# Gate and up projection of a decoder layer: column groups two at a time, with seven block products in place of eight in some units

## Chip, core and metric

One core of one Trainium2 chip runs the whole layer. The metric is the device time of one execution in microseconds (us), the median of several runs.

## What is computed

One decoder layer for 256 tokens with a model width of 2048, all in float32: a convolution branch and an attention branch, their joint output projection, and a gated feed-forward part.

```python
mix = concat([rmsnorm(u, conv_out_norm), rmsnorm(attn, attn_out_norm)]) @ w_out
x = x + rmsnorm(mix, post_mix_norm)
hf = rmsnorm(x, pre_ffn_norm)
ff = (silu(hf @ w_gate) * (hf @ w_up)) @ w_down      # 2048 -> 5632 -> 2048
x = x + rmsnorm(ff, post_ffn_norm)
```

## The kernel before

The 256 tokens are two token blocks (tb) of 128. Every float32 operand of a product is held as two float16 parts, hi and lo, and a product of one 128-row tile with 512 columns is three matmuls: hi times hi, hi times lo, lo times hi. A weight tile of 128x2048 float32 (1 MB) is loaded by SyncE's queue (SP) into one of 4 buffers `st`; `split` (L98 to L100) lets ScalarE write the hi part `whi` (L99) and then VectorE the lo part `wlo` (L100). The parts have 8 buffers each in the pool `wsp`. The tile framework fixes in advance the order in which each engine's instructions stand; an engine takes them in that order, so an instruction that waits holds up all behind it.

The output projection of the convolution half (L588 to L595) ends with x for the next part. For each tb, L601 adds the residual, L602 squares it for the norm, L604 forms x times the gain, L606 splits that, and L607 transposes the parts by DMA into `hf`. The norm's factor `r_f` (L610 to L612) is not in `hf`: it is applied to the product, as a scale in `swiglu` (L640, L645).

The gate and up projection (L661 to L677) has 22 column groups j of 512 columns (256 of gate, 256 of up) and 16 row tiles. A group's weights are 4 loads, its products 96 matmuls into two accumulators of the pool `acc` (4 PSUM banks). The first two groups do tb 0 before tb 1. `swiglu` computes silu(gate) times up, and splits and transposes it into `aT`. For the groups in `FAST` (0, 2, ..., 18) it also forms three differences of blocks, `sT`, for the down projection.

The down projection (L737 to L802) has 22 pairs of row tiles and two halves of 1024 columns. A pair is one load of four blocks, and a plain pair has eight block products (2 tb x 2 column groups x 2 row tiles, 24 matmuls). Ten pairs take seven (21 matmuls), the Strassen-Winograd form: the weights' four sums are formed in place on VectorE (L730 to L732) and split again, so VectorE has for such a pair a split of 128x1536, three additions and a split of 128x2048. Four products go into the pool `tmp` (the other 4 banks) and are added at the end of a half (L778 to L786). Fast and plain pairs alternate.

```python
nc.vector.tensor_tensor(st[:, 0:4:3, :], st[:, 0:2, :], st[:, 3:4, :].to_broadcast([P, 2, 512]), op=ALU.add)
nc.vector.tensor_tensor(st[:, 1, :], st[:, 0, :], st[:, 1, :], op=ALU.add)
nc.vector.tensor_tensor(st[:, 2, :], st[:, 1, :], st[:, 2, :], op=ALU.add)
return parts + parts_of(st, 2048)
```

Of the kernel before, what the change touches and what calls it, by code (L numbers as in the profile page):

```python
# [17 lines left out]
P = 128  # L18
# [33 lines left out]
def hymba_layer(ctx: ExitStack, tc: tile.TileContext, x, xT, pos, inv_freq, g_pre, w_in, w_lat,  # L52
# [15 lines left out]
    arena = const.tile([P, 70 * KB], F32, name="arena")  # L68
# [511 lines left out]

    mxc_of = flat(mx_h[:, :CB], mx_l[:, :CB])
    x_off = dram.tile([P, NTB, D], F32, name="x_off")
    r_f = const.tile([P, NTB], F32, name="r_f")
    for tb in range(NTB):
# [13 lines left out]
        for j in range(4):  # L598
# [25 lines left out]
    hw3 = region(50, (2, 3, P), F16)  # L624

# [3 lines left out]
    def fast_of(j):  # L629
# [5 lines left out]
    def swiglu(j, ps):  # L635
        fast = j in FAST
        for tb in range(NTB):
            r = r_f[:, tb : tb + 1]
            sg = work.tile([P, 256], F32, tag="A", name=nm("sg"), bufs=3)
            nc.scalar.activation(sg, ps[tb][:, 0:256], AF.Silu, scale=r)  # L640
# [4 lines left out]
            nc.vector.scalar_tensor_tensor(a, ps[tb][:, 256:512], r, sg, op0=ALU.mult, op1=ALU.mult)  # L645
# [15 lines left out]
    LEAD = 2  # L661
    lead = []
    for j in range(NG):
        wgt = Weights(KD, 512).load(w_gu[j], W_S)
        ps = [acc_tile(), acc_tile()]
        if j < LEAD:
            mm3(ps[0:1], hf_of, wgt, (0,))
            lead.append((wgt, ps))
            if j == LEAD - 1:
                for i, (wgt, ps) in enumerate(lead):  # L670
                    mm3(ps[1:2], hf_of, wgt, (1,))
                    swiglu(i, ps)
# [44 lines left out]
    def parts_of(st, n):  # L717
        hi = wsp.tile([P, 2048], F16, tag="whi", name=nm("whi"))
        lo = wsp.tile([P, 2048], F16, tag="wlo", name=nm("wlo"))
        split(hi[:, :n], lo[:, :n], st.rearrange("p b n -> p (b n)")[:, :n], WD_S)  # L720
        return [(hi[:, c : c + 512], lo[:, c : c + 512]) for c in range(0, n, 512)]

    def load_pair(u, i):

        st = stage.tile([P, 2048], F32, tag="stage", name=nm("st")).rearrange("p (b n) -> p b n", b=4)
        nc.sync.dma_start(st, w_dn[u, i])
        if i not in FAST:
            return parts_of(st, 2048)
        parts = parts_of(st, 1536)
        nc.vector.tensor_tensor(st[:, 0:4:3, :], st[:, 0:2, :], st[:, 3:4, :].to_broadcast([P, 2, 512]), op=ALU.add)  # L730
        nc.vector.tensor_tensor(st[:, 1, :], st[:, 0, :], st[:, 1, :], op=ALU.add)
        nc.vector.tensor_tensor(st[:, 2, :], st[:, 1, :], st[:, 2, :], op=ALU.add)  # L732
        return parts + parts_of(st, 2048)

# [150 lines left out]
```

## Time and profile before

| | |
|---|---|
| median of 3 runs | 1015.81 us (1015.81 to 1016.43) |
| profiled execution | 1016.03 us, span 1014.2 us, mean granted TensorE clock 0.991 |
| busy, share of the span | TensorE 96%, VectorE 73%, ScalarE 53% |
| HBM read | 204.25 MB, 206 GB/s over the span |

The span runs from the first to the last instruction; 1.8 us of the time lie around it. Busy shares are means over stages, so the stages have to be read apart: the gate and up projection lies between about 330 and 784 us, the down projection from there to about 1005 us.

### The profile page before, as it was taken

Reading aid. Unit: us, or ns where it says so; the run is one execution under the profiler, and the core shown is the slowest. Engines: PE = TensorE matmul, PEld = TensorE weight load, DVE = VectorE, ACT = ScalarE, POOL = GpSimd, SP = SyncE. Lnnn points to the kernel's source line nnn. Section 1 sums busy time; section 2 is a strip of 40 time slices with the busy share of each in tenths; the row PEclk is TensorE's granted clock in tenths of the full one; section 3 lists DMA queues with packets and bytes.
Section 4 is the critical chain, followed back from the end, with each engine's and each line's share of the span. In section 5 each row is a group of like instructions: output and inputs, shape, how many; then the busy total and the mean of one; then the engine's idle time right before and its main releaser. Section 6 shows DMA issues by size and latency. Waiting matters only on the chain.

```text
span 1014.2 us, 11941 instructions
## 1 busy us (share of the span) xinstructions
PE 975.7 (96%) x4652; PEld 462.3 (46%) x4652; DVE 742.5 (73%) x860; ACT 532.5 (53%) x599; POOL 37.7 (4%) x50
## 2 busy tenths in 40 slices
PE   6999997999999999999999999999999999989996
PEld 2444553774444444444444444444444444434442
DVE  6699999999868886555455555555556788888787
ACT  7796665664746564454444444454443544554551
POOL 0000000034100100000000000000000000000000
PEclk9999998999999999999999999999999999999998
DMA  9874666576546998676766776777755555635453
GB/s 348 330 256 140 223 209 196 166 241 222 201 166 170 321 303 290 218 228 201 240 217 206 222 224 223 226 218 217 234 198 166 176 189 224 235 127 222 166 186 145
DMA packets 77769, 220.37 MB, mean 217 GB/s; under 512 B 49552, under 2 KB 50192, under 8 KB 55184
## 3 DMA queue, kind: packets, MB, share of 16 engines
q1 hardware_dynamic: 76992, 218.68, 64.2%
q10 hardware_dynamic: 720, 0.93, 0.3%
q8 instruction: 36, 0.59, 0.2%
q14 instruction: 21, 0.17, 0.1%
HBM read 204.25 MB, written 4.19 MB: 206 GB/s over the span
## 4 chain that ended last, share of the span: by engine, by line
PE 64%; DVE 18%; issue 5%; ACT 5%; POOL 2%; DMA 1%; DVEq 0%; POOLq 0%; ACTq 0%; SPq 0%
PE acc L146 16%; PE acc L145 16%; PE acc L144 16%; DVE wlo L100 7%; DVE arena L277 3%; PE acc L749 3%; PE acc L750 3%; PE acc L748 3%; ACT whi L99 3%; DVE st L730 1%; PE tmp L749 1%; PE tmp L750 1%; PE tmp L748 1%; POOL sm L198 1%; DVE arena L285 1%
## 5 line engine op out<-in xcount | busy, mean ns | idle before, releaser
L100 DVE SCALAR_TENSOR_TENSOR wlo<-st,whi 128x2048 f16<-128x2048 f32 (+4 forms) x211 | 451.7, 2157 | 203.3 <-ACT whi L99 203.3
L99 ACT ACTIVATE whi<-st 128x2048 f16<-128x2048 f32 (+4 forms) x211 | 376.2, 1800 | 320.7 <-PE acc L146 176.5
L144 PE MATMUL acc<-whi,arena 128*128 128x512 f16 (+1 forms) x1084 | 410.1, 378 | 5.5 <-ACT whi L99 5.5
L145 PE MATMUL acc<-wlo,arena 128*128 128x512 f16 (+1 forms) x1084 | 410.4, 379 | 3.9 <-DVE wlo L100 3.8
L146 PE MATMUL acc<-whi,arena 128*128 128x512 f16 (+1 forms) x1084 | 409.8, 378 | 0.0
L144 PEld LDWEIGHTS <-arena 128*128 128x128 f16 x1084 | 106.7, 98 | 130.2 <-ACT arena L104 4.9
L146 PEld LDWEIGHTS <-arena 128*128 128x128 f16 x1084 | 106.7, 98 | 129.6 <-issue 6.9
L145 PEld LDWEIGHTS <-arena 128*128 128x128 f16 x1084 | 106.5, 98 | 125.2 <-issue 2.5
L748 PE MATMUL acc<-whi,arena 128*128 128x512 f16 x232 | 87.9, 379 | 0.0
L749 PE MATMUL acc<-wlo,arena 128*128 128x512 f16 x232 | 87.9, 379 | 0.0
L750 PE MATMUL acc<-whi,arena 128*128 128x512 f16 x232 | 87.9, 379 | 0.0
L277 DVE SCALAR_TENSOR_TENSOR arena<-arena 128x256 f32<-128x256 f32 x184 | 78.0, 480 | 0.0
L640 ACT ACTIVATE sg<-acc,r_f 128x256 f32<-128x256 f32 x44 | 20.7, 473 | 58.8 <-PE acc L146 58.8
L749 PEld LDWEIGHTS <-arena 128*128 128x128 f16 x272 | 26.6, 98 | 32.3 <-issue 0.3
L748 PEld LDWEIGHTS <-arena 128*128 128x128 f16 x272 | 26.6, 98 | 32.1
L750 PEld LDWEIGHTS <-arena 128*128 128x128 f16 x272 | 26.6, 98 | 32.1
L283 ACT ACTIVATE x_sb<-arena 128x256 f32<-128x256 f32 x56 | 25.2, 506 | 11.7 <-DVE arena L285 11.7
L705 POOL TENSOR_TENSOR sm<-sm,neg_half 128x1 f32<-128x1 f32 x2 | 1.1, 541 | 657.0 <-DVE sm L703 657.0
L730 DVE TENSOR_TENSOR st<-st 128x1024 f32<-128x1024 f32 x20 | 24.5, 1224 | 0.6
L153 PE MATMUL tmp<-arena,whi 128*128 128x256 f16 x80 | 21.8, 273 | 0.0
L154 PE MATMUL tmp<-arena,whi 128*128 128x256 f16 x80 | 21.8, 273 | 0.0
L155 PE MATMUL tmp<-arena,wlo 128*128 128x256 f16 x80 | 21.8, 273 | 0.0
(186 smaller groups left out, 610.1 us busy)
## 6 DMA issues: line engine op xcount, KB each, us to landing
st<-in_w_gu SPq DMA_DIRECT2D x88, 1024.0 KB, 5.0
st<-in_w_dn SPq DMA_DIRECT2D x44, 1024.0 KB, 4.9
st<-in_w_out SPq DMA_DIRECT2D x16, 1024.0 KB, 5.1
st<-in_w_in SPq DMA_DIRECT2D x14, 1024.0 KB, 9.3
st<-in_w_lat SPq DMA_DIRECT2D x12, 896.0 KB, 5.0
x_sb<-in_x SPq DMA_DIRECT2D x4, 1024.0 KB, 8.7
st<-in_w_uqn SPq DMA_DIRECT2D x4, 768.0 KB, 4.9
st<-in_w_uv SPq DMA_DIRECT2D x2, 1024.0 KB, 6.0
```

The lines of the kernel that those rows point to most:

```text
L99: nc.scalar.activation(hi, src, AF.Copy, scale=scale)
L100: nc.vector.scalar_tensor_tensor(lo, src, scale, hi, op0=ALU.mult, op1=ALU.subtract)
L144: nc.tensor.matmul(p_ap, xh, wh, start=(start and k == 0), stop=False)
L145: nc.tensor.matmul(p_ap, xh, wl, start=False, stop=False)
L146: nc.tensor.matmul(p_ap, xl, wh, start=False, stop=(stop and k == wgt.kt - 1))
L153: nc.tensor.matmul(ps, wh[:, c0 : c0 + P], xh, start=(k == 0), stop=False)
L277: nc.vector.scalar_tensor_tensor(cacc[:, cb, :], upad[:, cb, k : k + S], cw[:, cb, k : k + 1], cacc[:, cb, :], op0=ALU.mult, op1=ALU.add)
L283: nc.scalar.activation(t[:, i, :], upad[:, cb, k : k + S], AF.Copy, scale=cw[:, cb, k : k + 1])
L730: nc.vector.tensor_tensor(st[:, 0:4:3, :], st[:, 0:2, :], st[:, 3:4, :].to_broadcast([P, 2, 512]), op=ALU.add)
L748: nc.tensor.matmul(ps, ah, bh, start=key not in begun, stop=False)
L749: nc.tensor.matmul(ps, ah, bl, start=False, stop=False)
L750: nc.tensor.matmul(ps, al, bh, start=False, stop=last)
```

## The change

The gate and up projection takes its 22 column groups in 11 units of two, with weights laid out in blocks as for the down projection. In units 1, 3, 5, 7 and 9, five of the eight pairs of row tiles (0 to 4) take seven block products; pair 5 goes first, then 0 to 4, then 6 and 7. All other units have eight plain pairs. The down projection uses the same class and changes only in that its tail holds two pairs, not three. A unit's four results and, in a fast unit, its four sums fill all eight PSUM banks; units in turn take their results from `acc` and from `tmp`, and their sums from the other pool.

Sums of blocks of the normed input are needed too (`hf_sums`, once, in unit 0), and sums of blocks from two tb have to have the same scale, so the norm's factor now goes into `hf` itself (`normed`): a token block's squares are reduced and raised to the power before the first split.

```diff
+GU_UNITS = (1, 3, 5, 7, 9)
+GU_FAST = 5
...
+    def normed(tb, j):
+        cs = slice(j * 512, (j + 1) * 512)
+        gx = work.tile([P, 512], F32, tag="ss", name=nm("gxf"), bufs=3)
+        nc.vector.scalar_tensor_tensor(gx, x_sb[:, tb, cs], r_f[:, tb : tb + 1], g_pf[:, cs], op0=ALU.mult, op1=ALU.mult)
+        return gx
...
             nc.scalar.activation(junk_tile(512), xs, AF.Square, accum_out=ss4[:, j : j + 1])
-            gx = work.tile([P, 512], F32, tag="ss", name=nm("gxf"), bufs=3)
-            nc.vector.tensor_tensor(gx, xs, g_pf[:, cs], op=ALU.mult)
+        s1 = smalls()
+        nc.vector.tensor_reduce(s1, ss4, axis=AX.X, op=ALU.add)
+        rstd_of(s1, D, out_tile=r_f[:, tb : tb + 1])
+        for j in range(4):
             hl = work.tile([P, 2, 512], F16, tag="hl", name=nm("hl"))
-            split(hl[:, 0, :], hl[:, 1, :], gx, X_S)
+            split(hl[:, 0, :], hl[:, 1, :], normed(tb, j), X_S)
...
+    def hf_sums(c):
+        g0, g1 = [normed(tb, c).rearrange("p (i k t) -> p i k t", i=2, k=2) for tb in range(NTB)]
+        sm = region(44, (4, 2, P))
+        for d, p, m in ((0, g1[:, :, 0], g1[:, :, 1]), (1, g0[:, :, 0], g1[:, :, 0]),
+                        (2, g0[:, :, 0], sm[:, 0]), (3, g0[:, :, 1], sm[:, 2])):
+            nc.vector.tensor_tensor(sm[:, d], p, m, op=ALU.subtract)
+        hl = region(48, (2, 8 * P), F16)
+        split(hl[:, 0, :], hl[:, 1, :], sm.rearrange("p s i t -> p (s i t)"), X_S)
+        nc.sync.dma_start_transpose(hS[:, c], hl.rearrange("p a n -> p (a n)"))
...
+    class Unit:
+        def __init__(self, x_of):
+            mine, other = (acc_tile, tmp_tile) if Unit.count % 2 == 0 else (tmp_tile, acc_tile)
+            Unit.count += 1
+            self.E = [[mine(), mine()], [mine(), mine()]]
...
+        def fast(self, blocks, w, last):
+            if self.sums is None:
+                self.sums = [self.other() for _ in range(4)]
+            X, Y, Z, Q = self.sums
+            A22, A11, A12, S1, S3, S2, S4 = blocks
+            self.mm(self.E[0][0], (0, 0), A12, w[2])
+            self.mm(self.E[0][1], (0, 1), S4, w[1])
+            self.mm(X, "X", A11, w[0], last)
+            self.mm(Y, "Y", S2, w[4], last)
+            self.mm(Z, "Z", S3, w[6], last)
+            self.mm(Q, "Q", S1, w[3], last)
+            self.mm(self.E[1][0], (1, 0), A22, w[5])
+            if last:
+                xs_ = work.tile([P, 512], F32, tag="hl", name=nm("xs"))
+                nc.scalar.copy(xs_, X)
+                m, n_, q2 = [work.tile([P, 512], F32, tag="ss", name=nm(b), bufs=3) for b in ("m", "n", "q2")]
+                nc.vector.tensor_tensor(m, xs_, Y, op=ALU.subtract)
+                nc.vector.tensor_tensor(n_, m, Z, op=ALU.add)
+                nc.vector.tensor_tensor(m, Q, m, op=ALU.subtract)
+                nc.vector.tensor_tensor(q2, Q, n_, op=ALU.subtract)
+                self.fix = [[xs_, m], [n_, q2]]
+        def block(self, tb, c):
+            e = self.E[tb][c]
+            if self.fix is None:
+                return e
+            f = self.fix[tb][c]
+            nc.vector.tensor_tensor(f, e, f, op=ALU.add)
+            return f
...
+    gu_order = [GU_FAST] + list(range(GU_FAST)) + list(range(GU_FAST + 1, KP))
+    for u in range(NU):
+        unit = Unit(hf_of)
+        if u == 0:
+            ws = [load_pair(w_gu[u, i], W_S, False) for i in range(KP)]
+            for tb in range(NTB):
+                for i, w in enumerate(ws):
+                    for c in range(2):
+                        unit.plain(i, w, tb, c, i == KP - 1)
+                if tb == 0:
+                    for c in range((GU_FAST + 1) // 2):
+                        hf_sums(c)
         else:
-            mm3(ps, hf_of, wgt)
-            swiglu(j, ps)
+            order = gu_order if u in GU_UNITS else list(range(KP))
+            for i in order:
+                fast = u in GU_UNITS and i < GU_FAST
+                w = load_pair(w_gu[u, i], W_S, fast)
+                if fast:
+                    unit.fast(hf_fast(i), w, i == GU_FAST - 1)
+                else:
+                    unit.plain_all(i, w, i == order[-1])
+        for c in range(2):
+            swiglu(2 * u + c, unit, c)
...
-    TAIL = 3
+    TAIL = 2
```

`load_pair` and `parts_of` are moved from the down projection unchanged but for the scale; the reduced dynamic DMA scratch makes room for `hS`.

How the order of instructions moves, at three places. First VectorE in the middle of the gate and up projection: before, one column group of 512 (L645 and L655 are in `swiglu`, the rows with arena its splits).

```order
L100 SCALAR_TENSOR_TENSOR wlo_4604<-st_4601,whi_4603 128x2048
L100 SCALAR_TENSOR_TENSOR wlo_4610<-st_4607,whi_4609 128x2048
L100 SCALAR_TENSOR_TENSOR wlo_4616<-st_4613,whi_4615 128x2048
L645 SCALAR_TENSOR_TENSOR arena<-acc_4349,r_f,sg_4447 128x256
L645 SCALAR_TENSOR_TENSOR arena<-acc_4350,r_f,sg_4450 128x256
L655 TENSOR_TENSOR arena<-arena 128x128 x4
L100 SCALAR_TENSOR_TENSOR wlo_4622<-st_4619,whi_4621 128x2048
```

In the change, the end of unit 3's fast pairs (L676 to L678 are the additions that were L730 to L732, L105 the split, L730 and L731 the first steps of adding the four sums):

```order
L105 SCALAR_TENSOR_TENSOR wlo_3982<-st_3979,whi_3981 128x1536
L676 TENSOR_TENSOR st_3979<-st_3979 128x2x512
L677 TENSOR_TENSOR st_3979<-st_3979 128x512
L678 TENSOR_TENSOR st_3979<-st_3979 128x512
L105 SCALAR_TENSOR_TENSOR wlo_3989<-st_3979,whi_3988 128x2048
L105 SCALAR_TENSOR_TENSOR wlo_4016<-st_4013,whi_4015 128x1536
L676 TENSOR_TENSOR st_4013<-st_4013 128x2x512
L677 TENSOR_TENSOR st_4013<-st_4013 128x512
L678 TENSOR_TENSOR st_4013<-st_4013 128x512
L105 SCALAR_TENSOR_TENSOR wlo_4023<-st_4013,whi_4022 128x2048
L105 SCALAR_TENSOR_TENSOR wlo_4059<-st_4056,whi_4058 128x2048
L730 TENSOR_TENSOR m_4049<-xs_4047,acc_3887 128x512
```

Fast pairs stand one behind the other, with nothing between L678 and the split that follows it.

Second, VectorE where the gate and up projection ends and the weights of the down projection are prepared. Before (the accumulators of the last group are acc_5867 and acc_5868):

```order
L100 SCALAR_TENSOR_TENSOR wlo_6092<-st_6089,whi_6091 128x2048
L100 SCALAR_TENSOR_TENSOR wlo_6122<-st_6119,whi_6121 128x1536
L730 TENSOR_TENSOR st_6119<-st_6119 128x2x512
L731 TENSOR_TENSOR st_6119<-st_6119 128x512
L732 TENSOR_TENSOR st_6119<-st_6119 128x512
L645 SCALAR_TENSOR_TENSOR a_5967<-acc_5867,r_f,sg_5965 128x256
L645 SCALAR_TENSOR_TENSOR a_5975<-acc_5868,r_f,sg_5973 128x256
```

In the change (unit 10's results are acc_5919 to acc_5922, L757 is the multiplication of `swiglu`):

```order
L105 SCALAR_TENSOR_TENSOR wlo_6306<-st_6303,whi_6305 128x2048
L105 SCALAR_TENSOR_TENSOR wlo_6336<-st_6333,whi_6335 128x1536
L757 SCALAR_TENSOR_TENSOR a_6165<-acc_5919,sg_6163 128x256
L676 TENSOR_TENSOR st_6333<-st_6333 128x2x512
L105 SCALAR_TENSOR_TENSOR ahl_6167<-a_6165,ahl_6167 128x256
L757 SCALAR_TENSOR_TENSOR a_6173<-acc_5921,sg_6171 128x256
L757 SCALAR_TENSOR_TENSOR a_6181<-acc_5920,sg_6179 128x256
L677 TENSOR_TENSOR st_6333<-st_6333 128x512
L105 SCALAR_TENSOR_TENSOR ahl_6175<-a_6173,ahl_6175 128x256
L757 SCALAR_TENSOR_TENSOR a_6189<-acc_5922,sg_6187 128x256
```

The four reads that free the banks stand behind the split of seven weight tiles of the down projection (wlo_6204 is the first), and its first pair now takes its sums from `acc`, so from these four banks.

Third, VectorE where token block 0 is made ready. Before:

```order
L601 SCALAR_TENSOR_TENSOR x_sb<-arena,sm_2730,x_sb 128x512 x2
L604 TENSOR_TENSOR gxf_2736<-x_sb,arena 128x512
L604 TENSOR_TENSOR gxf_2745<-x_sb,arena 128x512
L601 SCALAR_TENSOR_TENSOR x_sb<-arena,sm_2730,x_sb 128x512 x2
L100 SCALAR_TENSOR_TENSOR hl_2738<-gxf_2736,hl_2738 128x512
```

In the change (L613 is the old L601, L603 the old L591, L616 the reduction of the squares, L590 is in `normed`):

```order
L613 SCALAR_TENSOR_TENSOR x_sb<-arena,sm_2730,x_sb 128x512 x4
L105 SCALAR_TENSOR_TENSOR wlo_2948<-st_2945,whi_2947 128x2048
L603 SCALAR_TENSOR_TENSOR arena<-acc_2776,r_c,arena 128x512
L105 SCALAR_TENSOR_TENSOR wlo_2954<-st_2951,whi_2953 128x2048
L105 SCALAR_TENSOR_TENSOR wlo_2960<-st_2957,whi_2959 128x2048
L616 TENSOR_REDUCE sm_2745<-sm_2732 128x1
L605 TENSOR_TENSOR arena<-arena 128x512
L201 TENSOR_SCALAR sm_2747<-sm_2745 128x1
L603 SCALAR_TENSOR_TENSOR arena<-acc_2805,r_c,arena 128x512
L590 SCALAR_TENSOR_TENSOR gxf_2751<-x_sb,r_f,arena 128x512
```

Three splits of weights and the norm's steps now stand between the finished x and the first normed tile; after this row two more rows of L590 and a fourth split of weights follow before the first `hl`.

## Rows read from the trace of the kernel before

**Rows 1.** The page, busy time of each engine over the span.
```profile
PE 975.7 (96%) x4652; PEld 462.3 (46%) x4652; DVE 742.5 (73%) x860; ACT 532.5 (53%) x599; POOL 37.7 (4%) x50
```

**Rows 2.** Windows: stretch, length, busy us per engine (instructions), PEclk, DMA share, GB/s.
```profile
330.00:351.00 21.00, 19.53 (x92) 8.76 (x91) 18.74 (x25) 10.16 (x18) 3.06 (x2) 1.00 1.02 333
351.00:784.00 433.00, 433.00 (x2008) 196.31 (x2007) 251.28 (x218) 198.39 (x171) 0.00 (x0) 1.00 0.71 227
784.00:892.00 108.00, 108.00 (x502) 48.95 (x501) 89.44 (x68) 52.44 (x35) 0.00 (x0) 1.00 0.53 197
892.00:896.00 4.00, 0.78 (x5) 0.29 (x3) 3.28 (x3) 3.39 (x5) 0.00 (x0) 1.00 0.02 4
896.00:1005.00 109.00, 107.07 (x495) 48.09 (x492) 88.83 (x73) 48.24 (x38) 0.54 (x1) 1.00 0.47 180
400.00:500.00 100.00, 100.00 (x465) 45.36 (x464) 54.58 (x48) 44.78 (x40) 0.00 (x0) 1.00 0.70 219
```

**Rows 3.** Waits, 340 to 735 us: who waited for whom, us, times, longest.
```profile
ACT whi L99 <- PE acc L146: 152.6, 55, 3.5
```

**Rows 4.** TensorE's timeline in the gate and up projection: start, us, what.
```profile
729.76 0.38 PE L144 MATMUL acc<-whi,arena 128*128 128x512 f16 x1
...
772.06 0.38 PE L145 MATMUL acc<-wlo,arena 128*128 128x512 f16 x1
```

**Rows 5.** VectorE's timeline in the down projection, one fast and one plain pair.
```profile
853.38 6.16 DVE L100 SCALAR_TENSOR_TENSOR wlo<-st,whi 128x2048 f16<-128x2048 f32 x3 [2.06 <-ACT whi L99]
859.58 1.23 DVE L730 TENSOR_TENSOR st<-st 128x1024 f32<-128x1024 f32 x1
860.84 0.69 DVE L731 TENSOR_TENSOR st<-st 128x512 f32<-128x512 f32 x1
861.56 0.69 DVE L732 TENSOR_TENSOR st<-st 128x512 f32<-128x512 f32 x1
864.31 10.56 DVE L100 SCALAR_TENSOR_TENSOR wlo<-st,whi 128x2048 f16<-128x2048 f32 x5 [2.06 <-ACT whi L99]
```

**Rows 6.** VectorE's groups by form, 740 to 1000 us: busy us, mean ns.
```profile
L784 DVE TENSOR_TENSOR m<-tmp,m 128x512 f32<-128x512 f32 x2 | 1.4, 686 | 0.1
L686 DVE TENSOR_TENSOR xs<-acc,xs 128x512 f32<-128x512 f32 x2 | 1.4, 688 | 1.0 <-PE acc L750 1.0
```

**Rows 7.** Where the input of the gate projection is made: timelines of VectorE and TensorE.
```profile
309.37 1.42 DVE L601 SCALAR_TENSOR_TENSOR x_sb<-arena,sm,x_sb 128x512 f32<-128x512 f32 x2 [0.66 <-POOL sm L198]
313.23 1.29 DVE L100 SCALAR_TENSOR_TENSOR hl<-gxf,hl 128x512 f16<-128x512 f32 x2
330.15 0.74 DVE L591 SCALAR_TENSOR_TENSOR arena<-acc,r_c,arena 128x512 f32<-128x512 f32 x1
346.65 0.38 PE L145 MATMUL acc<-wlo,arena 128*128 128x512 f16 x1 [1.47 <-DVE wlo L100]
```

**Rows 8.** The tile hl: its transposes by DMA, ns min/median/max on SP, and landing in us.
```profile
L607 SPq DMA_TRANSPOSE arena<-hl x8: 1242/1532/3357, 313.9 to 349.7; - x8
DMA to landing us min/median/max: 3.1/4.1/5.9
```

**Rows 9.** VectorE's timeline where the gate and up projection ends.
```profile
784.46 0.69 DVE L732 TENSOR_TENSOR st<-st 128x512 f32<-128x512 f32 x1
785.07 0.87 DVE L645 SCALAR_TENSOR_TENSOR a<-acc,r_f,sg 128x256 f32<-128x256 f32 x2
```

**Rows 10.** TensorE's timeline after the two longest waits shown.
```profile
163.00 0.47 PE L373 MATMUL tmp<-ident,kp 128*128 128x128 f32 x1 [6.25 <-DVE kp L372]
895.66 0.38 PE L748 MATMUL acc<-whi,x_sb 128*128 128x512 f16 x1 [3.22 <-DVE m L686]
```

**Rows 11.** Windows behind the wait of 6.25 us, columns as in rows 2.
```profile
160.00:165.00 5.00, 2.00 (x6) 0.84 (x7) 3.87 (x18) 4.29 (x10) 1.16 (x2) 0.54 0.42 152
165.00:170.00 5.00, 5.00 (x20) 2.20 (x19) 5.00 (x9) 2.10 (x3) 0.00 (x0) 0.78 0.65 116
```

More of the change, by code (lines that the diff above doesn't have):

```diff
@@ L67, in hymba_layer @@
     KB = 256
-    arena = const.tile([P, 70 * KB], F32, name="arena")
+    arena = const.tile([P, 82 * KB], F32, name="arena")
     def region(kb, shape, dtype=F32):
@@ new lines, in parts_of, with load_pair @@
+    def parts_of(st, n, scale):
+        hi = wsp.tile([P, 2048], F16, tag="whi", name=nm("whi"))
+        lo = wsp.tile([P, 2048], F16, tag="wlo", name=nm("wlo"))
+        split(hi[:, :n], lo[:, :n], st.rearrange("p b n -> p (b n)")[:, :n], scale)
+        return [(hi[:, c : c + 512], lo[:, c : c + 512]) for c in range(0, n, 512)]
+    def load_pair(src, scale, fast):
+        st = stage.tile([P, 2048], F32, tag="stage", name=nm("st")).rearrange("p (b n) -> p b n", b=4)
+        nc.sync.dma_start(st, src)
+        if not fast:
+            return parts_of(st, 2048, scale)
+        parts = parts_of(st, 1536, scale)
+        nc.vector.tensor_tensor(st[:, 0:4:3, :], st[:, 0:2, :], st[:, 3:4, :].to_broadcast([P, 2, 512]), op=ALU.add)
+        nc.vector.tensor_tensor(st[:, 1, :], st[:, 0, :], st[:, 1, :], op=ALU.add)
+        nc.vector.tensor_tensor(st[:, 2, :], st[:, 1, :], st[:, 2, :], op=ALU.add)
+        return parts + parts_of(st, 2048, scale)
@@ new lines, in hymba_layer, with mm, plain, plain_all @@
+    class Unit:
+        count = 0
+        def __init__(self, x_of):
+            mine, other = (acc_tile, tmp_tile) if Unit.count % 2 == 0 else (tmp_tile, acc_tile)
+            Unit.count += 1
+            self.x_of, self.other = x_of, other
+            self.E = [[mine(), mine()], [mine(), mine()]]
+            self.sums = None
+            self.begun = set()
+            self.fix = None
+        def mm(self, ps, key, a, b, last=False):
+            (ah, al), (bh, bl) = a, b
+            nc.tensor.matmul(ps, ah, bh, start=key not in self.begun, stop=False)
+            nc.tensor.matmul(ps, ah, bl, start=False, stop=False)
+            nc.tensor.matmul(ps, al, bh, start=False, stop=last)
+            self.begun.add(key)
+        def plain(self, i, w, tb, c, last=False):
+            self.mm(self.E[tb][c], (tb, c), self.x_of(2 * i, tb), w[0 if c == 0 else 3])
+            self.mm(self.E[tb][c], (tb, c), self.x_of(2 * i + 1, tb), w[2 if c == 0 else 1], last)
+        def plain_all(self, i, w, last=False):
+            for tb in range(NTB):
+                for c in range(2):
+                    self.plain(i, w, tb, c, last)
+        def fast(self, blocks, w, last):
[26 more added lines that the diff above has]
+            return f
@@ L715, in final @@
             (nc.sync if j % 2 == 0 else nc.scalar).dma_start(out[tb * P : (tb + 1) * P, cs], xs)
[L717 to L733, printed above, removed]
@@ L788, in hymba_layer @@
+        unit = Unit(a_of)
+        for i in order[:-TAIL]:
+            w = load_pair(w_dn[u, i], WD_S, i in FAST)
+            if i in FAST:
+                unit.fast(a_fast(i), w, i == FAST[-1])
+            else:
+                unit.plain_all(i, w)
+        tail = [(i, load_pair(w_dn[u, i], WD_S, False)) for i in order[-TAIL:]]
         if u == 1:
```

101 lines of the change are left out of this document (25 added, 76 removed).

## Prediction

> **What bounds the kernel now.** I read the page's busy shares first, then the windows by stage, then who waits for whom in each stage. Over the span TensorE is busy 96% and VectorE 73% [rows 1]; the windows show that this mean hides two kinds of stage [rows 2]. From 351 to 784 us TensorE has no gap, and VectorE is busy 54.58 us of 100: the gate and up projection is paced by TensorE, and ScalarE's hi splits wait for it to give back buffers, 152.6 us in 55 waits [rows 3]. From 784 us on VectorE is busy 89.44 of 108 us. There it also waits 2.06 us in each fast pair for ScalarE: the second hi split can start only when the last addition is done, and nothing else stands between them in VectorE's queue [rows 5]. The cadence of one fast and one plain pair is 864.31 - 853.38 = 10.93 us.
>
> TensorE's price is read from 197 matmuls in a row without a gap, (772.06 - 729.76) / 196 = 0.2158 us each [rows 4]. A plain pair (24) is 5.18 us, a fast pair (21) 4.53, a plain unit of eight 41.4. One fast and one plain pair are 9.71 us, so the down projection's VectorE is already 1.2 us slower per two pairs than its TensorE. It lives on the lead that it brings from the gate and up projection, and one wait for an evacuation shows (3.22 us, [rows 10]). The change carries such pairs to a stage where VectorE had time, and puts five of them in a row. The question is whether there is time enough.
>
> **What TensorE is spared.** Five units by five pairs by three matmuls are 75 matmuls (the order of the change has 150 TensorE rows fewer, a weight load and a matmul each): 75 x 0.2158 = 16.2 us. This is the whole gain, if TensorE stays the pace.
>
> **What VectorE pays in a fast unit and the plain one after it.** Two splits back to back of 128x2048 cost (10.56 - 6.16) / 2 = 2.2 us each [rows 5]. So a fast pair, ScalarE's wait with it, is 10.93 - 2.2 = 8.73 us where a plain pair is 2.2: 6.53 more. The first order piece shows the same wait bare again: L676 to L678, then at once the split that needs them. Before, two units (16 pairs) take 2 x 41.4 = 82.9 us of TensorE, in which VectorE is busy 0.5458 x 82.9 = 45.2. Now five fast pairs add 32.7 and the eight additions of the four sums 8 x 0.69 = 5.5 [rows 6]: 83.4 us. TensorE has 369 matmuls, 79.6. **VectorE alone is as long as the old pair of units**; the 16.2 us are gone before any wait is counted.
>
> One wait is sure to be added. The additions into the results (L742) wait for a unit's last product, and they stand in VectorE's queue after three more splits and the four steps of the sums. When the last fast pair's second split is done, TensorE still has 12 matmuls of it and two plain pairs, 60 x 0.2158 = 12.9 us; VectorE has 3 x 2.2 + 4 x 0.69 = 9.4. It stands 3.6 us at L742, with all splits of the next unit behind it. So two units take 83.4 + 3.6 = 87.0 instead of 82.9: +4.1, five times, **+20.5 us**. A walk through unit 3 agrees: counted from TensorE's start on it, VectorE has the second split of pairs 2, 3 and 4 ready at about 16.0, 24.6 and 33.2 us; TensorE asks for them at 16.1, 20.7 and 29.1, and so waits about 4 us twice. Bounds: below, 0.5 a cycle if the wait at L742 is covered; above, about 5, if ScalarE's queue holds up a split for a microsecond. I take 4.1, since every price in it is a row of the same operations in the same order.
>
> **The first fast unit** starts worse. In its place VectorE has the three `hf_sums`, each two passes of 512 columns, four of 256 and a split of 1024, about 4 us, while unit 0 still computes. In the later units VectorE has finished the second part of pair 1 about 2 us after TensorE starts on the unit; in unit 1 it then still has in front of it a split of 1024 (1.2), that pair's additions (2.7), the wait (2.06) and the split (2.2), with `swiglu` of unit 0 among them. I take **+7.4**, between 2 (the sums done while TensorE is late for other causes) and 11 (their whole cost).
>
> **Where hf is made.** Before, x is ready from 309.37 us, and the first split tile follows at 313.23 without the norm [rows 7]. Now the queue has between them, by the third order piece and the two more L590 and the split named behind it: four residuals (2.8), four splits of weights (8.9), six operations of 512 columns (4.2), the reduction and GpSimd's power (about 1.5): 309.4 + 17.4 = 326.8, the tile's own split to 327.5. A transpose lands 4.1 us after its issue [rows 8], 331.6; TensorE is through the output projection at 330.15 [rows 7]. So it starts 1.5 to 2 us late; I take 1.8. Token block 1 has the same longer chain behind two splits of weights: about 14 us from 338, landed at 355.6, when TensorE, 20.7 us (96 matmuls) after its start, asks at 352.5: 3.1 us, where before it waited 1.47 for a split [rows 7]. Sum **+3.4**, bounds 0 and 7: GpSimd's time for the power is the loosest part.
>
> **Where the down projection starts.** Before, VectorE comes to the last group's reads with no idle time at 785.07, just as the products end [rows 9], and the first pair uses other banks. Now its first pair needs unit 10's four banks after six matmuls (1.3 us), and the reads stand behind seven splits of the next weights. After its wait at unit 10's start VectorE has: four additions 2.8, `swiglu` 4.6 (two of the 20.7 us groups, 11.3 us busy each, less four splits), seven splits 15.4, two fast pairs 17.5, two plain 4.4, one first part 1.7: 46.4 us, against TensorE's 41.4. The first bank comes 46.4 + 0.45 - 42.7 = 4.2 us late. The second comes 2.5 us after it (an addition, a small split, two reads) where TensorE gives it 0.65, the last again 0.3 late: **+6.4**, bounds 2 and 10. From there to the end the down projection is as before; TAIL moves a plain pair into the loop, in the same place of TensorE's order, and the wait of 3.22 us between its halves may go, but VectorE then sets the end anyway.
>
> Units 1, 3, 5, 7, 9 start with a plain pair, 5.18 us in which the banks of the unit before are read out: no cost, covered by that pair; without it, the ladder of the last paragraph each time. Weight bytes do not change; a load lands while four are in hand.
>
> **Sum** against the profiled execution's 1016.03 us: 20.5 + 7.4 + 3.4 + 6.4 = 37.7, so 1053.7; the median shown is 0.2 below that execution: **1053.5 us**. A measurement of this kernel tells about 0.2% (2 us) from no change.
>
> **TensorE's clock.** Fast units bring gaps of about 4 us. After the wait of 3.22 us the granted clock stayed 1.00 [rows 2, 10]; after 6.25 us it was 0.54 and 0.78 in the next two stretches of 5 us, so partly the lower level of 1.2 GHz [rows 10, 11]. A gap of 4 us lies between, nearer the first, so I count no loss. The Trainium skill ("TensorE: Matmul & The Clock Gate", the section on HAM oscillation) says that gaps between groups of matmuls bring the clock back to half rate, so that each next group starts cold; by that rule the sum would be the second rival below.
>
> **Rivals.**
> - **TensorE stays the pace** (the other side). Should VectorE's work for two units fit under TensorE's 79.6 us, the stage gains 16.2; with 3.4 at the start and some 3 for the banks the time is 1016.0 - 16.2 + 6.4 = 1006 us. It decides at 8.0 us for a fast pair if the wait at L742 is covered, 7.3 if not. For it: the lead of eight buffers, and the row of 54.58% [rows 2]. Against it: 8.73 in every such pair of rows 5. 7%.
> - **The clock falls in the gaps.** In rows 11 the two stretches lost about 1 us each (2 us of running at 0.54, 5 at 0.78). Lost behind a unit's last gap, these 2.1 us come before L742 and so lengthen every cycle: 5 x 2.1 more, 1064 us. For it: two gaps of 4 us with only 4.5 us of work between. 10%.
> - **The loads become the pace.** Between fast units VectorE catches up at 2.2 us a tile; at 333 GB/s, the most in rows 2, a tile of 1 MB takes 3.1. Four or five tiles a cycle held up by 0.9 are 4 us, 20 in all: 1074. Against it: four tiles are in hand when it begins. 5%.
> - That the change does not do what it says is excluded: the order holds the 75 matmuls fewer.
>
> **How the numbers follow.** My case has 78%; its own range goes from 1016 + 14 = 1030 (the largest term at its lower end, 2.5, the other three at two thirds of what I take, 11.5) to 1016 + 53 = 1069 (all upper ends: 25, 11, 7, 10). The range 1030 to 1070 leaves out the first and last rival and some of the clock's. Faster by over 0.2% is the first rival, 0.07; within 0.2% needs VectorE at its lower bound everywhere and no late banks, 0.03; slower 0.90.
>
> **What would show it.** Right: VectorE busy some 84 us of 100 from 380 to 800 us (83.4 less five waits of 2.06, of 87.0), with ScalarE's waits for L678 (as now for L732) about 2 us before each second split, TensorE idle 6 to 8 us in each fast unit and waiting for `wlo` or `whi`, a wait of 3 to 4 us at L742, a gap of 4 to 6 us where the down projection starts. Wrong: no gaps in the fast units; a cycle near 80 us; or gaps that belong to loads, or a granted clock under 0.9 in the fast units.

## The result, and the profile after

The changed kernel takes 1049.55 us (median; 1048.13 to 1052.44), the kernel before 1016.12 beside it: a ratio of 1.0332, 95% interval 1.0309 to 1.0356. Forecast were 1053.5 us. The profiled execution took 1052.44 us, span 1050.6, 36.4 more than the span before. It is the slowest of the four executions; by the medians the change costs 33.4 us.

Busy time over the span, to be held against [rows 1]:

```profile
PE 978.4 (93%) x4577; PEld 458.4 (44%) x4577; DVE 874.0 (83%) x1019; ACT 567.7 (54%) x632; POOL 32.8 (3%) x50
```

TensorE has 75 matmuls fewer and is yet busy 2.7 us longer: some of them ran at the lower clock (granted 0.50 in the second window below). The windows by stage (columns as in rows 2):

```profile
326.00:332.00 6.00, 0.98 (x6) 0.25 (x5) 6.00 (x8) 2.86 (x4) 0.00 (x0) 0.93 1.05 254
332.00:338.00 6.00, 6.00 (x15) 2.15 (x16) 6.00 (x8) 2.59 (x5) 0.00 (x0) 0.50 0.97 323
...
376.00:427.00 51.00, 40.38 (x161) 16.65 (x160) 38.40 (x38) 23.30 (x20) 0.00 (x0) 0.90 0.54 153
427.00:470.00 43.00, 43.00 (x201) 19.50 (x200) 35.46 (x35) 20.91 (x18) 0.00 (x0) 1.00 0.77 271
470.00:514.00 44.00, 38.28 (x169) 16.62 (x167) 35.62 (x37) 23.09 (x21) 0.00 (x0) 0.96 0.48 163
...
814.00:922.00 108.00, 107.80 (x499) 48.65 (x498) 88.90 (x70) 52.22 (x37) 0.00 (x0) 1.00 0.58 211
922.00:940.00 18.00, 11.12 (x36) 4.10 (x35) 15.44 (x17) 9.39 (x12) 0.00 (x0) 0.72 0.33 122
```

Where one stretch of 433 us without a gap stood in rows 2, the fast units (376 to 427, 470 to 514) now have gaps and the plain units between them none. Who waits for whom, 320 to 835 us (us, times, longest), against [rows 3]:

```profile
ACT whi L104 <- DVE st L678: 125.7, 26, 6.4
DVE wlo L105 <- ACT whi L104: 73.0, 37, 3.5
ACT whi L104 <- DMA st<-in_w_gu: 61.3, 33, 5.0
```

ScalarE's wait for TensorE's buffers, 152.6 us before, is gone but for 3.0 us. In its place stand the additions (L678; of the 26 waits 25 are those of the projection's fast pairs) and, not foreseen in this size, the loads, for which ScalarE waited once before (340 to 735 us):

```profile
ACT whi L99 <- DMA st<-in_w_gu: 3.0, 1, 3.0
```

TensorE's timeline in the change shows where its time goes:

```profile
331.97 0.61 PE L699 MATMUL acc<-whi,arena 128*128 128x512 f16 x1 [5.02 <-DMA arena<-hl]
332.37 0.63 PE L700 MATMUL acc<-wlo,arena 128*128 128x512 f16 x1
332.80 0.63 PE L701 MATMUL acc<-whi,arena 128*128 128x512 f16 x1
...
407.05 1.44 PE L699 MATMUL acc<-whi,arena 128*128 128x512 f16 x3 [3.20 <-ACT whi L104]
...
925.72 0.38 PE L699 MATMUL tmp<-whi,x_sb 128*128 128x512 f16 x1 [1.38 <-DVE m L742]
930.07 0.58 PE L699 MATMUL tmp<-whi,x_sb 128*128 128x512 f16 x1 [3.54 <-DVE n L742]
933.47 0.58 PE L699 MATMUL tmp<-whi,arena 128*128 128x512 f16 x1 [1.96 <-DVE q L742]
```

The starts of the stages on TensorE divide the 36.4 us. The start of the gate and up projection, unit 0 with it, costs 6.5. Units 1 and 2 together take 96.3 us in place of 82.9 (+13.4), the four cycles of two units behind them 87.7, 88.0, 83.8 and 82.0 (+9.9), the down projection 236.4 in place of 230.05 (+6.3).

Why the cycles are long is seen on ScalarE and VectorE between two fast units (unit 4 runs from 518.93 to 560.37):

```profile
536.36 1.91 ACT L104 ACTIVATE whi<-st 128x2048 f16<-128x2048 f32 x1 [4.75 <-DMA st<-in_w_gu]
538.31 2.29 DVE L105 SCALAR_TENSOR_TENSOR wlo<-st,whi 128x2048 f16<-128x2048 f32 x1 [3.42 <-ACT whi L104]
...
544.25 1.76 DVE L105 SCALAR_TENSOR_TENSOR wlo<-st,whi 128x1536 f16<-128x1536 f32 x1 [1.19 <-ACT whi L104]
```

The window over it, with PEclk, the DMA share and GB/s at its end:

```profile
536.00:541.00 5.00, 5.00 (x25) 2.28 (x24) 2.52 (x2) 3.82 (x2) 0.00 (x0) 1.00 1.02 426
```

In the plain unit, where VectorE should catch up, it has no tile for 3.42 us and again for 1.19, while the DMA engines are busy at 426 GB/s in the window shown.

### The profile page after: what moved, and what is told of

It is laid out like the page before. It is cut to its first block, busy times and chain, and to the rows that moved or that the text cites. A ratio compares the mean times of both kernels' runs of the same rounds, so it can differ in the third digit from the quotient of the medians.

```text
span 1050.6 us, 11954 instructions
## 1 busy us (share of the span) xinstructions
PE 978.4 (93%) x4577; PEld 458.4 (44%) x4577; DVE 874.0 (83%) x1019; ACT 567.7 (54%) x632; POOL 32.8 (3%) x50
## 4 chain that ended last, share of the span: by engine, by line
DVE 33%; PE 33%; issue 11%; ACT 9%; DMA 8%; POOL 1%; SPq 0%; DVEq 0%; ACTq 0%; POOLq 0%
DVE wlo L105 14%; ACT whi L104 7%; DMA st<-in_w_gu 5%; PE acc L700 4%; PE acc L701 4%; PE acc L699 4%; PE tmp L701 3%; PE tmp L700 3%; PE tmp L699 3%; DVE arena L282 3%; DVE st L676 3%; PE acc L151 2%; PE acc L150 2%; PE acc L149 2%; DVE st L678 2%
## 5 line engine op out<-in xcount | busy, mean ns | idle before, releaser
L105 DVE SCALAR_TENSOR_TENSOR wlo<-st,whi 128x2048 f16<-128x2048 f32 (+4 forms) x236 | 492.5, 2114 | 111.5 <-ACT whi L104 111.5
L104 ACT ACTIVATE whi<-st 128x2048 f16<-128x2048 f32 (+4 forms) x236 | 409.4, 1764 | 314.0 <-DVE st L678 211.6
L699 PE MATMUL acc<-whi,arena 128*128 128x512 f16 x620 | 237.1, 385 | 20.4 <-ACT whi L104 13.7
L700 PE MATMUL acc<-wlo,arena 128*128 128x512 f16 x620 | 239.7, 387 | 10.9 <-DVE wlo L105 10.8
L701 PE MATMUL acc<-whi,arena 128*128 128x512 f16 x620 | 239.6, 386 | 0.0
L149 PE MATMUL acc<-whi,arena 128*128 128x512 f16 (+1 forms) x380 | 143.5, 378 | 5.9 <-ACT whi L104 5.9
L150 PE MATMUL acc<-wlo,arena 128*128 128x512 f16 (+1 forms) x380 | 143.5, 378 | 2.4 <-DVE wlo L105 2.3
L151 PE MATMUL acc<-whi,arena 128*128 128x512 f16 (+1 forms) x380 | 143.6, 379 | 0.0
L699 PE MATMUL tmp<-whi,arena 128*128 128x512 f16 x331 | 126.3, 385 | 3.1 <-DVE q L742 2.0
L700 PE MATMUL tmp<-wlo,arena 128*128 128x512 f16 x331 | 127.0, 384 | 0.0
L701 PE MATMUL tmp<-whi,arena 128*128 128x512 f16 x331 | 126.6, 383 | 0.0
L149 PEld LDWEIGHTS <-arena 128*128 128x128 f16 x380 | 37.7, 99 | 47.4 <-ACT arena L109 5.2
L676 DVE TENSOR_TENSOR st<-st 128x1024 f32<-128x1024 f32 x45 | 55.0, 1222 | 1.2
L678 DVE TENSOR_TENSOR st<-st 128x512 f32<-128x512 f32 x45 | 31.1, 691 | 1.4
L677 DVE TENSOR_TENSOR st<-st 128x512 f32<-128x512 f32 x45 | 31.1, 691 | 1.4
```

Source lines behind the costliest of these rows:

```text
L104: nc.scalar.activation(hi, src, AF.Copy, scale=scale)
L105: nc.vector.scalar_tensor_tensor(lo, src, scale, hi, op0=ALU.mult, op1=ALU.subtract)
L149: nc.tensor.matmul(p_ap, xh, wh, start=(start and k == 0), stop=False)
L150: nc.tensor.matmul(p_ap, xh, wl, start=False, stop=False)
L151: nc.tensor.matmul(p_ap, xl, wh, start=False, stop=(stop and k == wgt.kt - 1))
L699: nc.tensor.matmul(ps, ah, bh, start=key not in self.begun, stop=False)
```

## Experiments

The theory when they began was that of the forecast: VectorE's chain of split, additions, ScalarE's hi part and second split is too long for TensorE's time, and the rest is small. What the runs have to compare is VectorE's first read of a unit's results in `swiglu` (the multiplication, L757) for units 2, 4, 6 and 8, and the steps between them, two units each:

| run | unit 2 | steps to units 4, 6, 8 |
|---|---|---|
| the change | 475.34 | 86.4, 86.6, 85.0 |
| additions left out | 455.99 | 79.6, 79.6, 79.6 |
| units 3, 5, 7, 9 | 458.60 | 80.9, 81.5, 80.9 |
| no sums of hf | 467.01 | 86.3, 87.0, 86.0 |
| half loads | 472.24 | 88.3, 80.4, 80.6 |
| loads from GpSimd | 476.21 | 89.8, 87.7, 82.0 |

TensorE's own time for two units is 369 x 0.2158 = 79.6 us.

**The restructuring alone** (no fast pair in the gate and up projection):

```diff
-GU_UNITS = (1, 3, 5, 7, 9)
-GU_FAST = 5
+GU_UNITS = ()
+GU_FAST = 0
```

> The gate and up projection in units of two column groups with the norm inside hf, but no fast pair and no sums of hf. Theory (VectorE's work for fast pairs is the cost; the new layout costs only where hf is made): 1016 plus the 6.5 us that the changed kernel's TensorE loses before unit 1, so 1022 us, between 1019 and 1025, with no gap in TensorE from there to the down projection. Rival (the four results of a unit and the swap of banks cost time themselves): 1030 or more, with gaps at the units' ends.

Measured: 1026.13 us, ratio 1.0095 (1.008 to 1.011). This is 1.1 us above the theory's range. Its TensorE waits over 0.2 us only where hf is made and between the halves of the down projection, and the theory had left out the second place:

```profile
331.87 0.61 PE L699 MATMUL acc<-whi,arena 128*128 128x512 f16 x1 [5.17 <-DMA arena<-hl]
903.74 0.59 PE L699 MATMUL tmp<-whi,x_sb 128*128 128x512 f16 x1 [3.54 <-DVE n L742]
907.14 0.59 PE L699 MATMUL tmp<-whi,arena 128*128 128x512 f16 x1 [1.96 <-DVE q L742]
```

So about 10 us of the loss have nothing to do with fast pairs in this projection: they lie with the norm's longer chain ahead of hf, and with the banks that are read between the halves of the down projection.

**The additions left out**, in the gate and up projection alone, so that its fast pairs multiply unsummed weights, as in the next run:

```diff
-        nc.vector.tensor_tensor(st[:, 0:4:3, :], ...)
-        nc.vector.tensor_tensor(st[:, 1, :], ...)
-        nc.vector.tensor_tensor(st[:, 2, :], ...)
+        if scale == WD_S:
+            ...
```

> The changed kernel without the three additions of weight blocks in the gate and up projection; the second split takes the blocks as loaded, so the output is not the layer's. Theory (VectorE sets the pace of the fast units): VectorE's fast pair falls from 8.7 to 3.95 us, below TensorE's 4.5, TensorE sets the pace again and the 16.2 us of spared matmuls show: 1016 + 6.5 - 16.2 = 1006 us, up to 1012 where the sums of hf still delay unit 1. Rival (loads, banks or the clock set the pace, not VectorE): 1030 or more.

Measured: 1010.97 us, 0.9947 (0.9932 to 0.9962).

**The additions made, but into a scratch tile that nobody reads**; the second split takes the blocks as they were loaded:

```diff
...
+        else:
+            jk = junk_tile(1024).rearrange("p (b n) -> p b n", b=2)
+            nc.vector.tensor_tensor(jk, st[:, 0:2, :], st[:, 3:4, :].to_broadcast([P, 2, 512]), op=ALU.add)
+            nc.vector.tensor_tensor(jk[:, 0, :], st[:, 0, :], st[:, 1, :], op=ALU.add)
+            nc.vector.tensor_tensor(jk[:, 1, :], st[:, 1, :], st[:, 2, :], op=ALU.add)
```

> The changed kernel with the same three additions on VectorE, written to a scratch tile, while the second split takes the blocks as loaded, so ScalarE no longer waits for the additions; the output is not the layer's. Theory (work and wait together make 8.7 us): 6.6 us a fast pair, some 73 us of VectorE in two units where TensorE has 79.6, so nearly all the loss goes: 1008 to 1018 us. Rival (the additions' own 2.6 us already suffice, the wait is covered): 1035 or more.

Measured: 1008.95 us, 0.993 (0.9913 to 0.9946). Busy time of this run:

```profile
PE 963.2 (96%) x4577; PEld 455.8 (45%) x4577; DVE 869.5 (86%) x1019; ACT 569.8 (57%) x632; POOL 37.6 (4%) x50
```

VectorE does nearly all its work (869.5 us against 874.0) and the time is that of the run without it. The additions as work alone cost nothing; with the wait that they force they cost 40 us.

**Unit 1 plain**, four fast units left:

```diff
-GU_UNITS = (1, 3, 5, 7, 9)
+GU_UNITS = (3, 5, 7, 9)
```

> The changed kernel with fast pairs in units 3, 5, 7 and 9 only; the sums of hf are still made in unit 0. Theory (unit 1 is slow because those sums stand in VectorE's queue just before it): units 1 and 2 fall back to 82.9 us from the 96.3 of the changed kernel's trace, and unit 3 takes about 46 us, so 1049.5 - 13.4 = 1036 us, between 1032 and 1040. Rival (the first fast unit is slow because it is the first, whatever stands before it): unit 3 then takes 52 to 55 us and the time is 1042 or more.

Measured: 1015.02 us, 0.9986 (0.9977 to 0.9995). It lies 17 us below the nearer theory's range: one fifth of the fast pairs held as much as the whole loss. The steps are 81 us here, and TensorE has no wait between 331.67 and 723 us. ScalarE's waits, 376 to 815 us, show a kind that the change does not have at all in this stretch:

```profile
ACT whi L104 <- DVE st L678: 132.3, 24, 8.4
ACT whi L104 <- DMA st<-in_w_gu: 39.7, 32, 4.3
ACT whi L104 <- PE acc L701: 9.4, 4, 3.3
ACT whi L104 <- PE tmp L701: 5.8, 2, 3.3
```

Six times ScalarE waits for TensorE to give back a buffer: all eight are full, VectorE is ahead as far as it can be. The new theory was VectorE's **lead**, the split tiles that it has ready when TensorE asks for them: a fast unit is affordable only to a VectorE that comes to it with full buffers, and one that comes without never gets them back.

**Unit 1 fast again, unit 3 plain**:

```diff
-GU_UNITS = (1, 3, 5, 7, 9)
+GU_UNITS = (1, 5, 7, 9)
```

> Four fast units as in the run with units 3, 5, 7 and 9 (1015.0 us), but unit 1 is fast again and units 2, 3 and 4 are plain. Theory, the lead: a fast unit costs VectorE more than TensorE takes for it, and what was lost in unit 1 (54.9 us in the changed kernel where a fast unit without a wait takes 38.2) is won back in the three plain units behind it, so that units 5, 7 and 9 run without waits again: 1015 + 13 (units 1 and 2 took 96.3 us instead of the 82.9 of before) = 1028 us, 1024 to 1032. Rival: each fast unit costs some 8 us by its own waits, whatever stands ahead of it, and the run with units 3, 5, 7 and 9 was an exception of its order: 1040 us or more.

Measured: 1030.56 us, 1.0147 (1.0132 to 1.0162), inside the lead's range. TensorE waits in unit 1 as before and then nowhere until the halves of the down projection meet. The buffers are full again ten times:

```profile
ACT whi L104 <- PE tmp L701: 18.8, 6, 3.3
...
ACT whi L104 <- PE acc L701: 9.4, 4, 3.3
```

So the fast pairs cost 15.5 us more in unit 1 than in unit 3 (1030.56 - 1015.02). Three plain units in a row win the lead back, which the theory's "never" did not allow for; one does not.

**Without the sums of hf** (the fast pairs take tiles of hf in their place):

```diff
-                    for c in range((GU_FAST + 1) // 2):
-                        hf_sums(c)
+                    pass
```

> The changed kernel without the sums of hf: the fast pairs of the gate and up projection multiply tiles of hf that are there already in place of the sums, so about 13 us of VectorE's work ahead of unit 1 is left out, and the output is not the layer's. Theory A, the sums take VectorE's lead: unit 1 finds the lead that the others would have, VectorE's 81 us for two units against TensorE's 79.7 then cost little: 1012 to 1025 us. Theory B, the place takes it: unit 0 goes through its weights twice and holds all eight buffers of split weights until its second pass, so that VectorE cannot work ahead for unit 1, with or without sums: 1040 us or more.

Measured: 1041.51 us, 1.026 (1.0239 to 1.0281), in the range of theory B. The sums are worth 8 us, all in front of unit 2 (475.34 to 467.01 in the table), and the steps behind stay at 86. The place of the fast unit, directly behind unit 0, is most of it; that unit 0's two passes over its eight tiles are the reason was not tried by itself.

**A plain pair first in each half of the down projection**, with units 3, 5, 7 and 9:

```diff
-    order = [i for f, s in zip(FAST, slow) for i in (f, s)] + slow[len(FAST) :]
+    order = [i for f, s in zip(FAST, slow) for i in (s, f)] + slow[len(FAST) :]
```

> Fast units 3, 5, 7 and 9 as in the run of 1015.0 us, and each half of the down projection starts with a plain pair in place of a fast one. Theory: the waits of 1.34, 3.54 and 1.96 us between the halves come from the fast pair's eight banks, whose reads VectorE makes one after the other at the end of the first half; a plain pair ahead needs four of them only, so most of the 6.84 us and the half clock after them go: 1007 us, 1004 to 1010. Rival: VectorE is the pace of the down projection, and what TensorE doesn't wait between the halves it waits later: 1013 to 1016 us.

Measured: 1016.44 us, 1.0004 (0.9995 to 1.0014), just above the rival's range. TensorE's timeline has other waits between the halves (5.0 us in five, the first two of them shown; with the fast pair first they were 6.84 in three), and then one for VectorE in each pair of pairs:

```profile
886.28 0.38 PE L699 MATMUL acc<-whi,arena 128*128 128x512 f16 x1 [1.80 <-ACT xs L728]
889.13 0.38 PE L699 MATMUL acc<-whi,arena 128*128 128x512 f16 x1 [1.40 <-DVE m L730]
...
958.09 0.38 PE L700 MATMUL tmp<-wlo,x_sb 128*128 128x512 f16 x1 [1.06 <-DVE wlo L105]
```

**The transposes of `swiglu` from ScalarE's queue**, in the changed kernel:

```diff
-            nc.sync.dma_start_transpose(aT[...], hl...)
+            nc.scalar.dma_start_transpose(aT[...], hl...)
```

(and the two for the groups in `FAST`)

> The changed kernel with the transposes of swiglu issued from ScalarE's queue in place of SyncE's, where the loads of the weights stand behind them. Theory: in the changed kernel the four transposes of a unit hold the next loads up until 531.21 us in the unit from 518.93, and VectorE then has no tile for 3.0 to 4.8 us in each two units; with the loads free, two units take VectorE's 81 us and not 85.4: about 4 x 4 us, 1034 us, 1030 to 1040. Rival: the load is late because its buffer is late, not because of the queue: 1046 to 1052 us. If ScalarE stands waiting for the parts that it is to transpose, with hi splits behind it: 1055 us or more.

Measured: 1074.14 us, 1.0592 (1.0562 to 1.0622). It says nothing of the loads, since ScalarE became late itself. The waits from 433 to 815 us: VectorE waits for ScalarE up to 11.4 us in one piece, and for 25.0 us ScalarE waits for nothing that the profile shows, so for its own queue:

```profile
DVE wlo L105 <- ACT whi L104: 67.3, 30, 11.4
ACT whi L104 <- DMA st<-in_w_gu: 45.4, 28, 11.8
ACT whi L104 <- issue: 25.0, 4, 6.8
```

**Half the bytes in the loads of plain pairs**, in the changed kernel:

```diff
+        if not fast and scale == W_S:
+            nc.sync.dma_start(st[:, 0:2, :], src[:, 0:2, :])
+            ...
+            half = st[:, 0:2, :].rearrange("p (o b) n -> p o (b n)", o=1).to_broadcast([P, 2, 1024])
+            split(hi.rearrange("p (o n) -> p o n", o=2), lo.rearrange("p (o n) -> p o n", o=2), half, scale)
+            ...
```

> The changed kernel with half the bytes in each plain pair's load of the gate and up projection: two blocks are loaded and split twice, so that the splits and products stay as many and as long, and the output is not the layer's. Theory: with VectorE without a lead, the plain pairs are taken as fast as they land; a load of 1 MB lands about 5 us after a late issue, and VectorE stands 3.0 to 4.8 us in each two units. With half the bytes most of that goes: 1034 us, 1030 to 1040. Rival: the issue is late, behind the transposes, and half the bytes land only some 1.5 us sooner, once in two units: 1042 to 1048 us. If loads are not the cause: 1048 to 1052.

Measured: 1035.45 us, 1.0186 (1.0166 to 1.0206). In the plain unit VectorE now has four splits without a gap and then one of 1.45 us:

```profile
524.10 8.89 DVE L105 SCALAR_TENSOR_TENSOR wlo<-st,whi 128x2048 f16<-128x2048 f32 x4
534.43 1.76 DVE L105 SCALAR_TENSOR_TENSOR wlo<-st,whi 128x1536 f16<-128x1536 f32 x1 [1.45 <-ACT whi L104]
```

The last two steps fall to 80.5 us. Only plain tiles were lightened, and with them the whole excess over VectorE's 81 is gone there. Two reservations: about 3 of the 14 us are won before unit 2's results are read (472.24 in place of 475.34 in the table, TensorE's start on the projection being 2.75 us sooner), and VectorE's waits for TensorE's results (L742 in the change) are gone from these steps as well, so the run does not price the loads apart from them. (The first step stays at 88.3; why was not followed up. The order of VectorE's queue shifts by a few rows too.)

**The loads from GpSimd's queue**, in the changed kernel:

```diff
-        nc.sync.dma_start(st, src)
+        (nc.gpsimd if scale == W_S else nc.sync).dma_start(st, src)
```

> The changed kernel with the loads of the gate and up projection issued from GpSimd's queue, which is nearly empty there, so that they no longer stand behind the four transposes of a unit on SyncE's queue; nothing else is changed in the text (the run with the transposes on ScalarE's queue could not show it, since ScalarE then waited). Theory, the queue: the 3.0 to 4.8 us in which VectorE has no tile go: 1034 us, 1030 to 1040. Rival, the transfers: 1045 to 1052. If GpSimd's own work on each load makes it late: over 1052.

Measured: 1051.8 us, 1.0345 (1.0317 to 1.0372), where the rival put it. A queue of their own wins the loads nothing, and VectorE still stands. They wait for VectorE's splits, as they did in SyncE's queue. The waits from 376 to 815 us, in this run and in the change:

```profile
POOL st L672 <- DVE wlo L105: 279.4, 56, 12.3
...
SPq L672 <- DVE wlo L105: 276.8, 66, 9.8
```

VectorE's timeline in the plain unit 4:

```profile
542.36 2.29 DVE L105 SCALAR_TENSOR_TENSOR wlo<-st,whi 128x2048 f16<-128x2048 f32 x1 [5.04 <-ACT whi L104]
```

A load can start only when VectorE has split the tile that lies in its buffer, and a fast tile keeps one of the four buffers for a whole chain. When the plain tiles come, the loads start one per split, and several are on their way at once.

This does not clear the transposes. In the change, the tile for which VectorE waited 3.42 us was the first load issued behind the four transposes of a unit: the split that freed its buffer ended at 527.94 (525.66 + 2.28), and the load was issued at 531.21. The same holds of the longest such wait in units 6 and 8. SyncE's timeline in the change:

```profile
527.42 3.75 SPq L762 DMA_TRANSPOSE arena<-ahl  x2
531.21 12.20 SPq L672 DMA_DIRECT2D st<-in_w_gu  x6
```

In the run with GpSimd's queue the load behind the 5.04 us was issued at 530.54 and took 9.8 us to land, and a transpose issued at 530.24 took 9.9. So freeing the queue alone wins nothing, but what the transposes cost the loads, in the queue or on the way, stays open.

**Nine fast pairs in a half of the down projection**, with units 3, 5, 7 and 9; and the same with the plain pair first:

```diff
-FAST = tuple(range(0, 20, 2))
+FAST = tuple(range(0, 18, 2))
```

> Fast units 3, 5, 7 and 9 as in the run of 1015.0 us, and nine fast pairs in a half of the down projection in place of ten. TensorE gets 6 matmuls more (1.3 us), VectorE 13.1 us less (2 x 6.53). Theory: VectorE is the pace of the down projection, and the 6.84 us between the halves and the low clock behind them are its lateness: about 8 less the 1.3: 1009 us, 1007 to 1012. Rival: the wait between the halves comes from eight banks that are read one after the other, at whatever lead: 1015 to 1017.

> As the run with nine fast pairs in a half of the down projection, and each half starts with a plain pair. Theory: the waits that appeared later in the second half when a plain pair came first (1.0 us in each pair of pairs, VectorE's pace of 10.93 us against 9.71) go with the fast pair that is dropped, and so do those between the halves: 1008 us, 1005 to 1011. Rival: VectorE has the pace in either case: 1014 us or more.

Measured: 1008.91 us, 0.9927 (0.9915 to 0.994), and **1005.35 us, 0.9895 (0.9881 to 0.9908)**, the fastest of all and faster than both kernels. TensorE's waits of the second kernel from 320 us to the end are two:

```profile
331.66 0.61 PE L699 MATMUL acc<-whi,arena 128*128 128x512 f16 x1 [4.95 <-DMA arena<-hl]
971.13 0.38 PE L700 MATMUL tmp<-wlo,x_sb 128*128 128x512 f16 x1 [1.06 <-DVE wlo L105]
```

TensorE has six matmuls more; VectorE has 13.1 us less by the forecast's 6.53 a pair, waits counted (its busy time falls by 9.3 us, 848.5 to 839.2). The time falls with VectorE's, so VectorE paced the down projection. With ten, the order of a half only moved the waits; with nine, it removes those between the halves.

## Why the prediction was right, point by point

- **What bounds it.** Right: with the chain of a fast pair VectorE, not TensorE, sets the pace. The run with the additions aside shows that the work alone fits, and that it takes the wait with it to pass TensorE's time, as the forecast priced it (2.06 us of the 8.73; the changed kernel's cadence, from one L676 of the trace to the next, is 554.75 - 546.04 = 8.71).
- **VectorE's 83.4 us for two units.** 81.1 where nothing hinders it (steps of the run with units 3, 5, 7, 9). Near; but that is 1.5 us more than TensorE's 79.6, and by itself it did not make the cycles long: with it TensorE had no wait in that run from 331.67 to 723 us.
- **3.6 us at L742.** This step failed in its size. L742's first addition needs only the unit's first result, whose last product comes 18 matmuls, 3.9 us, before the unit's end. In the three steps from unit 2 to unit 8 VectorE waited there 1.14, 2.41 and 0 us. The longest:

```profile
605.88 0.69 DVE L742 TENSOR_TENSOR n<-tmp,n 128x512 f32<-128x512 f32 x1 [1.90 <-PE tmp L701]
```

  The larger part is the **loads**: in the same steps VectorE waited 4.8 us (3.42 + 0.17 + 1.19, shown above), 3.6 and 3.3 for tiles of plain pairs. That is the mechanism of my third rival (5%), with 2.2 us at which VectorE takes a tile, though at 426 GB/s, not 333. I held it off with "four tiles are in hand when it begins", and they do not last: VectorE empties four buffers in four splits. It is also my own sign of being wrong, gaps that belong to loads. Four cycles at +4.1 each were forecast at 16.4 and gave 9.9.
- **The first fast unit, +7.4.** Units 1 and 2 gave +13.4, where +7.4 and one cycle's 4.1 were forecast. The sums were a cause (8 us), but the forecast saw the cost as paid once. The run from unit 3 shows that it is not: with the lead, VectorE's waits in the same steps beyond those for the additions are 0.55 us at most, and without it the later cycles wait for loads. That is how one unit's fast pairs come to hold 34 us (1049.55 - 1015.02).
- **Where hf is made, +3.4.** Measured 6.5. The chain was right (the tile landed for 331.97, forecast 331.6); TensorE's end was not. The 330.15 of [rows 7] is VectorE's read; the last matmul of the output projection starts at 326.57. The wait was 5.02, not 1.8 us, and the clock then stood at 0.50 for 6 us (15 matmuls where 28 fit). The second wait, forecast at 3.1, did not come. So +3.4 was too little, and its two halves were wrong in opposite ways.
- **Where the down projection starts, +6.4.** +6.3, by chance: at 814 us there is no wait. The loss is between the halves, where I thought that a wait might go. The banks of the first half are read with splits between them:

```profile
924.99 0.68 DVE L742 TENSOR_TENSOR m<-tmp,m 128x512 f32<-128x512 f32 x1
...
927.12 2.29 DVE L105 SCALAR_TENSOR_TENSOR wlo<-st,whi 128x2048 f16<-128x2048 f32 x1 [0.73 <-ACT whi L104]
929.33 0.68 DVE L742 TENSOR_TENSOR n<-tmp,n 128x512 f32<-128x512 f32 x1
```

  TensorE goes on at 930.07, right behind the read at 929.33, and loses 6.9 us in three waits where [rows 10] had 3.22 in one. The clock behind them (0.72 from 922 to 940) holds most of the rest.
- **The clock, counted at nothing.** Partly wrong: 0.50 behind the wait of 5.02 us, 0.90, 0.96 and 0.92 in units 1, 3 and 5, 0.72 between the halves. In unit 1 the slow matmuls lie mostly ahead of the next wait, which may take them in; what the low clock cost in the fast units was not tried. The Trainium skill's rule ("TensorE: Matmul & The Clock Gate", on HAM oscillation, that gaps between groups of matmuls bring the clock back to half rate) agrees with the wait of 5.02 us; units 7 and 9 kept 1.00 over gaps up to 1.95 us.

The sum, 37.7 against 36.4 in the profiled execution (33.4 by the medians), is better than its terms, and that is luck: too much in the later cycles stood against too little in the first unit and at hf.

## What to carry to other kernels

Work that is moved to an engine with idle time has to be priced by its chain, waits included, and then by the lead with which that engine arrives: the same fast pairs cost 15.5 us more in unit 1 than in unit 3. Ask what limits catching up (here the loads: four buffers, emptied at 2.2 us a tile, where 1 MB at 426 GB/s takes 2.5) and not only the mean. Where two engines are near balance, give back a little of the saving (one fast pair a half here) before reordering: reordering alone only moved the waits.

## What the runs showed of the hardware that was not expected

- The DMA engines moved 426 GB/s at a share of 1.02 (536 to 541 us) while three to four tiles were being loaded; the most in rows 2 is 333. The Trainium skill ("DMA: Bandwidth & Descriptors", "Where 436 GB/s comes from") gives a ceiling of 435 for the ports and has about 358 bind for HBM; with one core at work this trace goes by the first.
- A gap of 5.02 us left matmuls 0.43 us apart for 6 us (332.80 - 332.37). Short gaps do not tell it by their length: in unit 1 two of 1.52 and 1.95 us were followed by seven matmuls 0.43 us apart, in unit 7 two of 1.90 and 1.95 us by none, and behind 3.22 us alone [rows 10] the granted clock was 1.00 [rows 2].
- A transpose issued by ScalarE held its queue for 1.3 to 1.4 us in the median (three kinds, 1.2 to 3.3 us in all); moving the eight of two units there made the changed kernel 24.6 us slower.
- A load of 1 MB and a transpose issued 0.3 us apart took 9.8 and 9.9 us to land, where the median of the run's loads was 6.0.
